# A two-layer float32 trunk: the order of its first loads, the place of a split before the down projection, and the engine of a layer norm's affine step

## The chip, the cores and the metric

One core of one Trainium2 chip runs the program. The metric is the device time of one execution in microseconds (us), as the median of several runs; smaller is better.

## The reference

The input is x with 256 positions of 2048 features, in float32. Two layers follow one another, each with a mixer and a feed-forward part, both with a residual add.

```
h = rms_norm(x, mix_norm[0]);  p = h @ ab_w_in                # 2048 x 6144
x = x + concat(band_attention(q, k, v, bias), b * conv(c * hv)) @ ab_w_out
x = x + (silu(g @ w_gate) * (g @ w_up)) @ w_down               # g = rms_norm(x, ffn_norm[0]), hidden width 5632
u, v = split(gelu(rms_norm(x, mix_norm[1]) @ c_w_in))          # 2048 x 4096
v = (v - mean) * rsqrt(var + eps) * ln_g + ln_b                # layer norm over the 2048 features
x = x + (u * (w_s @ v + b_s)) @ c_w_out
x = x + feed-forward as above, second weights
out = rms_norm(x, final_norm)
```

## The kernel before

**Matmuls in three terms.** Each float32 operand is split into a high part (a cast to FP32R on ScalarE) and a low part (the operand minus the high part, on VectorE). `three` (lines 478 to 481) issues three matmuls for each product: high by high (L479), high by low (L480), low by high (L481). The activations are the stationary operand (128 by 128), the weights the moving one (512 columns).

**Steps.** The whole program is a list of steps. A "std" step is one chunk of `RC` = 4 blocks of 128 contraction rows by 512 weight columns, 1 MB; it takes 4 blocks x 2 row halves x 3 terms = 24 matmuls. `load(t)` (L184) brings the weights of step t into one of three `raw` buffers on SyncE's (SP's) queue; `prep(t)` (L268) makes `whi` and `wlo` from them in two halves, `cast_half` (L258, ScalarE) and `low_part` (L264, VectorE), into two buffers each. `end_step(t)` (L521) calls `load(t + LOAD_AHEAD)` with `LOAD_AHEAD` = 4, and then `prep(t + PREP_AHEAD)` with `PREP_AHEAD` = 2, which loads step t + 2 itself if nothing has:

```
load(t + LOAD_AHEAD)
prep(t + PREP_AHEAD)
```

Phases follow each other in this list: ab_in (48 steps), ab_out, up0, down0, c_in, c_out, up1, down1.

**The start** (lines 614 to 666). Loads stand in the program in this order: half of x0, half of step 0's weights, the other half of x0, the other half of the weights, x1, step 1 (by `prep(1)`), x2, x3. Between them stand the split of step 0 in two halves of two blocks and the transposes of x (`x_transposes`, L395: eight TensorE transposes (L385) for one x block of 512 features, then `xh` on ScalarE and `xl` on VectorE). `later(dt, fn)` puts a piece of work into the program dt half steps later; `x_transposes` of x2 and x3 come at half steps 1 and 3. GpSimd (POOL) issues the loads of the norm vectors and of the attention bias (`load_bias`, L656).

**Order of instructions.** The tile framework orders each engine's instructions with its own model of time, except where `manual_schedule` holds ScalarE and VectorE to program order: here from the start to half step 9, and in `run_mixed` from its third step to its end.

**Up phases** (`run_mixed`, L537). Eight steps make one block of 512 hidden features, 11 blocks a phase; the steps' kinds are `MIX` = "NNSNSNSN". An S step uses sums of weight blocks, `tt` (`combine_first`, L228), and extra parts `ha`, `la`; these lie in the pool `mixw`, and the transposed activations in the pool `forms`. `WINDOWS` writes out which ScalarE and VectorE work goes into which step. At a block's end the PSUM banks are added up by VectorE in `first`, `end_a1`, `end_a2` and `end_b` (all through `add`, L864). After the last step of a phase the manual order is closed, `handover` (L905) closes both pools, opens `x_next` and `split`, and splits the first hidden tile with `hT.split(0)` (`jh` L208 on ScalarE, `jl` L209 on VectorE), and then `prep(hi_t + 1)` and the last block's `end_b`, `gate`, `product` follow. The down phase accumulates in two of the banks that `end_b` reads.

**Layer norm** (`layer_norm`, L954, in phase c_in). After mean and variance, each of eight blocks of `vt` (128 x 512) gets three VectorE instructions: (a + mu) * rs (L980, where `mu` is the negative mean), times `lng` (L984), plus `lnb` (L985). `spatial` (L990) multiplies the result on TensorE.

Of the kernel before, what the change touches and what calls it, by code (L numbers as in the profile page):

```python
# [16 lines left out]
P = 128  # L17
S = 256
# [57 lines left out]
def trunk_kernel(  # L76
# [35 lines left out]
    def close_pool(*names):  # L112
        for name in names:
            sides.pop(name).close()
# [69 lines left out]
    def load(t):  # L184
        if t >= len(steps) or t in raws:
            return
        s = steps[t]
        r = wpool.tile([P, RC, NB], F32, tag="raw", name="raw", bufs=RAW_BUFS)
        raws[t] = r

        def part(dst, w, c0, k, n):
            nc.sync.dma_start(
                dst, w[k * P : (k + n) * P, c0 : c0 + NB].rearrange("(k p) n -> p k n", p=P)
            )

        if s.kind != "std":
            for side, (w, c0) in enumerate(s.src):
                part(r[:, side::2, :], w, c0, s.k0, 2)
            return
        (w, c0), = s.src  # L200
        if t:
            part(r, w, c0, s.k0, RC)
        else:
            part(r[:, 0:2, :], w, c0, 0, 2)
            return lambda: part(r[:, 2:4, :], w, c0, 2, 2)

    def split(hi, lo, src):
        nc.scalar.copy(hi, src)  # L208
        nc.vector.tensor_tensor(out=lo, in0=src, in1=hi.bitcast(F32), op=ALU.subtract)  # L209
# [93 lines left out]
    def load_x(n, h=None):  # L303
        a, b = (0, NB) if h is None else (h * NB // 2, (h + 1) * NB // 2)
        nc.sync.dma_start(xs[n][:, :, a:b], xv[:, :, n * NB + a : n * NB + b])
# [57 lines left out]
    def rsqrt(dst, src):  # L363
        nc.gpsimd.tensor_tensor(out=dst, in0=src, in1=mhalf[:, : src.shape[1]], op=ALU.pow)
# [27 lines left out]
    def gain_col(st, c):  # L392
        return vcol(st.gain, c) if st.cols is None else st.cols[:, c : c + 1]

    def x_transposes(st, n):  # L395
        if st.mixed:
            for i in (2 * n, 2 * n + 1):
                x_forms(st, xs[n], i)
            return
        hi = st.pool[0].tile([P, 4, S], F32R, tag=f"xh{n}", name=f"xh{n}")  # L400
        lo = st.pool[0].tile([P, 4, S], F32R, tag=f"xl{n}", name=f"xl{n}")
        for half in range(2):
            pt = transpose_pair(xs[n], half * 2 * P)
            cols = [4 * n + half * 2 + j for j in range(2)]
            for j, c in enumerate(cols):
                nc.scalar.activation(
                    hi[:, c % 4, :], pt[:, j * S : (j + 1) * S], AF.Copy, scale=gain_col(st, c)
                )
            for j, c in enumerate(cols):
                nc.vector.scalar_tensor_tensor(  # L410
                    out=lo[:, c % 4, :], in0=pt[:, j * S : (j + 1) * S], scalar=gain_col(st, c),
                    in1=hi[:, c % 4, :].bitcast(F32), op0=ALU.mult, op1=ALU.subtract,
                )
        st.hi[n], st.lo[n] = hi, lo

    def x_forms(st, src, i):

# [116 lines left out]
        "N": ((2, NA11, "b", 1), (2, NA12, "b", 3), (5, NA21, "b", 0), (5, NA22, "b", 2),  # L534
              (3, NS3, "b", 0), (3, NS5, "b", 2), (4, NA21, "b", 1), (4, NA22, "b", 3)),
    }
    def run_mixed(pi, lhs, ends, handover):  # L537


        mixed[0] = True  # L540
        order = ExitStack()
        lo_t = cur[0]
        hi_t = lo_t
        while hi_t < len(steps) and steps[hi_t].pi == pi:
            hi_t += 1
        n = len(MIX)
        ps, seen, left = {}, set(), {}
        block_end = [None]

        def window(t, text):  # L550
            for word in text.split():
                op, _, dt = word.partition("+")
                tt = t + int(dt or 1)
                if op in ("c0", "c1", "s0", "s1", "s"):
                    if tt < hi_t and tt not in done:
                        (cast_half if op[0] == "c" else low_part)(tt, op[1:])
                elif dt:
                    if tt < hi_t:
                        assert steps[tt].kind == "S"
                        {"t1": combine_first, "t2": combine_rest, "ha": prep_a_hi,  # L560
                         "la": prep_a_lo}[op](tt)
                elif block_end[0] and op in block_end[0]:
                    block_end[0].pop(op)()

        done = set(parts)
        for t in range(lo_t, hi_t):
            if t == lo_t + 2:
                order.enter_context(
                    tc.manual_schedule(
                        engines={mybir.EngineType.Activation, mybir.EngineType.DVE}  # L570
                    )
                )
            s = steps[t]
            i = s.k0 // 2
            pre, _, post = WINDOWS[i].partition(":")
            window(t, pre)
            jobs_due(2 * t)
            if s.first:
                seen = set()
                left = {}  # L580
                for kind in MIX:
                    for q in PRODUCTS[kind]:
                        left[q[0]] = left.get(q[0], 0) + 1
            for j, (q, fa, group, slot) in enumerate(PRODUCTS[s.kind]):
                if j == 4:
                    jobs_due(2 * t + 1)
                if q not in seen:
                    ps[q] = bank(BANKS[q])
                hi, lo = (parts_a if group == "a" else parts)[t]
                left[q] -= 1  # L590
                three(ps[q], lhs.hi[i][:, fa, :], lhs.lo[i][:, fa, :], hi[:, slot, :],
                      lo[:, slot, :], q not in seen, left[q] == 0)
                seen.add(q)
            now[0] = 2 * t + 2
            if i == MIX.rindex("S"):
                block_end[0] = ends(s.key, ps)
            window(t, post)
            parts_a.pop(t, None)
            del parts[t]
            cur[0] += 1  # L600
            load(t + LOAD_AHEAD)
            if t + 2 == hi_t:
                prep(t + 2)
        order.close()
        handover()
        prep(hi_t + 1)
        for op in ("end_b", "gate", "product"):
            block_end[0].pop(op)()
        mixed[0] = False
# [16 lines left out]
    load_x(0, 1)  # L626
    load_second()
    load_x(1)
    hi0 = wpool.tile([P, RC, NB], F32R, tag="whi", name="whi", bufs=W_BUFS)
    lo0 = wpool.tile([P, RC, NB], F32R, tag="wlo", name="wlo", bufs=W_BUFS)  # L630
    for h in range(2):
        sl = slice(2 * h, 2 * h + 2)
        split(hi0[:, sl, :], lo0[:, sl, :], raws[0][:, sl, :])
        x_transposes(st, h)
    parts[0] = (hi0, lo0)
    prep(1)
    for n in (2, 3):
        load_x(n)
        later(2 * n - 3, lambda n=n: x_transposes(st, n))
    for n in range(4):  # L640
        later(3 + n, lambda n=n: squares(st, n))
# [21 lines left out]
        nc.gpsimd.memset(bt[0:CH, :, 0:CH], NEG)  # L663
        biases[g] = bt

    load_bias(0)

    def scaled(ps, dst):
        for m in range(M):
# [146 lines left out]
        else:  # L816
            grp["c", g] = dst

    def open_mixed():
        mixw[0] = open_pool("mixw", "left")  # L820
        xpool[0] = open_pool("forms", "left")

    def end_mix_a():
        close_pool("mix_a", "x_a")
        open_mixed()

    run(0, st, ab_in_evac)
    later(5, end_mix_a)
# [4 lines left out]
    class Hidden:  # L833
# [6 lines left out]
        def new(self, n):  # L840
            self.f[n] = self.pool.tile([P, 4, S], F32, tag=f"h{n}", name=f"h{n}")
            return self.f[n]

        def split(self, n):
            hi = self.split_pool.tile([P, 4, S], F32R, tag="jh", name="jh", bufs=2)
# [4 lines left out]
    def ffn(pi, st, nst):  # L850
# [52 lines left out]
                        product=product)  # L903

        def handover():  # L905
            close_pool("forms", "mixw")
            xpool[0] = open_pool("x_next", "left")
            hT.split_pool = open_pool("split", "left")
            operand[pi + 1] = hT
            hT.split(0)  # L910

        run_mixed(pi, st, ends, handover)
        if nst:
            run(pi + 1, hT, lambda n, ps: residual_evac(nst, n, ps))
        else:
# [16 lines left out]
    lnb = mpool.tile([P, D], F32, name="lnb")  # L932
    nc.gpsimd.dma_start(lng, c_ln_g[0:1, :].broadcast_to([P, D]))
    nc.gpsimd.dma_start(lnb, c_ln_b[0:1, :].broadcast_to([P, D]))
    ws = mpool.tile([P, G, P], F32, name="ws")
    nc.gpsimd.dma_start(ws, c_w_s[0].rearrange("g t s -> t g s"))
    wsT = mpool.tile([P, G, P], F32, name="wsT")
    vt = mpool.tile([P, M, D], F32, name="vt")
# [15 lines left out]
    def layer_norm():  # L954
# [17 lines left out]
        )  # L972
        rs = small.tile([P, M], F32, tag="rs", name="rs")
        rsqrt(rs, var)
        for n in range(4):
            sl = slice(n * NB, (n + 1) * NB)

            def block(m, sl=sl):
                a = vt[:, m, sl]
                nc.vector.tensor_scalar(  # L980
                    out=a, in0=a, scalar1=mu[:, m : m + 1], scalar2=rs[:, m : m + 1],
                    op0=ALU.add, op1=ALU.mult,
                )
                nc.vector.tensor_tensor(out=a, in0=a, in1=lng[:, sl], op=ALU.mult)  # L984
                nc.vector.tensor_tensor(out=a, in0=a, in1=lnb[:, sl], op=ALU.add)  # L985

            for m in range(M):
                later(1 + 2 * n + m, lambda m=m, block=block: block(m))
# [51 lines left out]

    def end_mix_c():
        close_pool("mix_c", "x_next")
        open_mixed()

    run(4, st_c, c_in_evac)
    later(5, end_mix_c)
# [62 lines left out]

    ffn(6, st_g, None)  # L1110
    drain()
    close_pool("x_next", "ffn")


# [28 lines left out]
```

## Time and profile before

| what | value |
|---|---|
| device time, median of 3 runs (lowest to highest) | 2102.51 us (2102.01 to 2103.68) |
| device time of the profiled execution | 2104.71 us |
| its span in the profile | 2102.7 us |
| TensorE matmul (PE) busy | 2080.8 us, 99% |
| VectorE (DVE) busy | 1503.7 us, 72% |
| ScalarE (ACT) busy | 1115.7 us, 53% |
| GpSimd (POOL) busy | 17.8 us, 1% |
| moved by DMA | 404.80 MB, 193 GB/s in the mean |

Durations in the profile belong to the one profiled execution; 2104.71 us is its own device time, and its span leaves out what lies around it. PE, DVE, ACT, POOL and SP stand for the five engines, PEld for TensorE's weight loads. "[1.85 <-ACT whi L258]" behind an instruction means that its engine stood idle for 1.85 us before it, until ScalarE had finished `whi` at line 258. Matmuls are pipelined: one's busy time runs into the next one's, so the pace is read from their starts.

### The profile page before, as it was taken

How to read it: one execution, taken by the hardware profiler on the slowest of the kernel's cores; microseconds unless marked ns; L12 is line 12 of the kernel's file. 1: busy time of each engine (PE TensorE's matmuls, PEld its weight loads, DVE VectorE, ACT ScalarE, POOL GpSimd, SP SyncE). 2: the span in 40 equal slices, each digit the busy share in tenths (PEclk: the TensorE clock that was granted, in tenths of full speed). 3: DMA queues.
4: the chain of work that ended last, by engine and by line, in shares of the span. 5: the costliest groups of instructions: out<-in, count | busy, mean ns of one | idle time of the engine just before them, and what ended most of it. 6: DMA issues, size and time to landing. Idle time of an engine off the chain costs nothing.

```text
span 2102.7 us, 24018 instructions
## 1 busy us (share of the span) xinstructions
PE 2080.8 (99%) x9356; PEld 1719.7 (82%) x9356; DVE 1503.7 (72%) x1597; ACT 1115.7 (53%) x1318; POOL 17.8 (1%) x37
## 2 busy tenths in 40 slices
PE   8999999999999999999999999999999999999998
PEld 6888888888888888788888878888888888878886
DVE  4445555788888888766664475588888888876675
ACT  5444445655555555556554534565555555555554
POOL 1000000000000000000000000000000000000000
PEclk9999999999999999999999999999999999999999
DMA  6554555565555555655555655556555655565554
GB/s 236 178 187 161 185 196 180 187 204 190 201 196 203 200 192 191 246 183 200 182 199 182 199 162 178 183 190 208 181 200 200 209 191 200 200 200 200 190 191 140
DMA packets 205345, 404.80 MB, mean 193 GB/s; under 512 B 9420, under 2 KB 10032, under 8 KB 204976
## 3 DMA queue, kind: packets, MB, share of 16 engines
q1 hardware_dynamic: 203296, 397.45, 55.8%
q0 software_dynamic: 1328, 4.77, 0.7%
q8 instruction: 73, 1.20, 0.2%
q10 hardware_dynamic: 608, 1.06, 0.1%
q14 instruction: 40, 0.33, 0.0%
HBM read 401.14 MB, written 2.10 MB: 192 GB/s over the span
## 4 chain that ended last, share of the span: by engine, by line
PE 96%; DMA 1%; DVE 1%; ACT 1%; issue 1%; SPq 0%; POOLq 0%; POOL 0%; ACTq 0%; DVEq 0%
PE b L481 31%; PE b L480 31%; PE b L479 31%; PE b L385 2%; DMA raw<-in_ab_w_in_dram 1%; PE b L421 0%; PE b L997 0%; DVE wlo L264 0%; ACT whi L258 0%; PE b L689 0%; ACT junk L965 0%; DVE vt L984 0%; DVE vt L980 0%; PE b L733 0%; PE b L721 0%
## 5 line engine op out<-in xcount | busy, mean ns | idle before, releaser
L264 DVE TENSOR_TENSOR wlo<-raw,whi 128x1024 fp32r<-128x1024 f32 x618 | 728.3, 1219 | 278.5 <-ACT whi L258 278.3
L258 ACT CAST whi<-raw 128x1024 fp32r<-128x1024 f32 x618 | 618.4, 1050 | 431.4 <-PE b L481 309.2
L480 PE MATMUL b<-wlo,fh 128*128 128x512 f32 x1144 | 449.2, 393 | 0.0
L481 PE MATMUL b<-whi,fl 128*128 128x512 f32 x1144 | 445.5, 389 | 0.0
L479 PE MATMUL b<-whi,fh 128*128 128x512 f32 x1144 | 380.6, 391 | 0.0
L481 PE MATMUL b<-whi,jl 128*128 128x512 f32 x704 | 274.3, 391 | 0.8 <-DVE jl L209 0.8
L480 PE MATMUL b<-wlo,jh 128*128 128x512 f32 x704 | 274.4, 390 | 0.4 <-DVE wlo L264 0.4
L480 PE MATMUL b<-wlo,xh 128*128 128x512 f32 x640 | 252.8, 395 | 2.9 <-DVE wlo L264 2.9
L479 PE MATMUL b<-whi,jh 128*128 128x512 f32 x704 | 249.8, 391 | 2.6 <-DVE sg L864 2.6
L481 PE MATMUL b<-whi,xl 128*128 128x512 f32 x640 | 251.5, 393 | 0.0
L481 PEld LDWEIGHTS b<-whi,fl 128*128 128x128 f32 x1144 | 214.9, 188 | 43.5
L480 PEld LDWEIGHTS b<-wlo,fh 128*128 128x128 f32 x1144 | 214.8, 188 | 43.4
L479 PEld LDWEIGHTS b<-whi,fh 128*128 128x128 f32 x1144 | 213.2, 188 | 45.1
L479 PE MATMUL b<-whi,xh 128*128 128x512 f32 x640 | 243.3, 399 | 1.9 <-ACT whi L258 1.9
L209 DVE TENSOR_TENSOR jl<-h,jh 128x1024 fp32r<-128x1024 f32 x88 | 107.8, 1225 | 148.5 <-ACT jh L208 148.5
L258 ACT CAST whi<-tt 128x1024 fp32r<-128x1024 f32 x132 | 134.7, 1052 | 124.9 <-PE b L481 96.2
L208 ACT CAST jh<-h 128x1024 fp32r<-128x1024 f32 x88 | 92.8, 1054 | 200.1 <-PE b L480 200.0
L264 DVE TENSOR_TENSOR wlo<-tt,whi 128x1024 fp32r<-128x1024 f32 x132 | 157.2, 1220 | 56.1 <-ACT whi L258 56.1
L479 PEld LDWEIGHTS b<-whi,jh 128*128 128x128 f32 x704 | 132.2, 188 | 31.1 <-ACT whi L258 3.4
L481 PEld LDWEIGHTS b<-whi,jl 128*128 128x128 f32 x704 | 132.6, 188 | 29.2 <-DVE jl L209 1.7
L480 PEld LDWEIGHTS b<-wlo,jh 128*128 128x128 f32 x704 | 132.6, 188 | 28.1 <-DVE wlo L264 0.8
L480 PEld LDWEIGHTS b<-wlo,xh 128*128 128x128 f32 x640 | 121.6, 190 | 28.9 <-DVE wlo L264 4.2
(148 smaller groups left out, 2054.8 us busy)
## 6 DMA issues: line engine op xcount, KB each, us to landing
raw<-in_ffn_w_gate_dram SPq DMA_DIRECT2D x176, 512.0 KB, 3.6
raw<-in_ffn_w_up_dram SPq DMA_DIRECT2D x176, 512.0 KB, 4.5
raw<-in_ffn_w_down_dram SPq DMA_DIRECT2D x88, 1024.0 KB, 4.9
raw<-in_ab_w_in_dram SPq DMA_DIRECT2D x47, 1024.0 KB, 5.0
raw<-in_c_w_in_dram SPq DMA_DIRECT2D x32, 1024.0 KB, 5.2
raw<-in_ab_w_out_dram SPq DMA_DIRECT2D x16, 1024.0 KB, 4.8
raw<-in_c_w_out_dram SPq DMA_DIRECT2D x16, 1024.0 KB, 4.9
x<-in_x_dram SPq DMA_DIRECT2D x3, 512.0 KB, 11.8
```

Source lines behind the costliest of these rows:

```text
L208: nc.scalar.copy(hi, src)
L209: nc.vector.tensor_tensor(out=lo, in0=src, in1=hi.bitcast(F32), op=ALU.subtract)
L258: nc.scalar.copy(parts[t][0][:, HALF[h], :], r[:, HALF[h], :])
L264: nc.vector.tensor_tensor(out=lo[:, sl, :], in0=r[:, sl, :], in1=hi[:, sl, :].bitcast(F32), op=ALU.subtract)
L385: nc.tensor.transpose(out=pt[:, j * S + m * P : j * S + (m + 1) * P], in_=src[:, m, c0 + j * P : c0 + (j + 1) * P], identity=ident,)
L479: nc.tensor.matmul(ps, lhsT=ah, rhs=bh, start=start, stop=False)
L480: nc.tensor.matmul(ps, lhsT=ah, rhs=bl, start=False, stop=False)
L481: nc.tensor.matmul(ps, lhsT=al, rhs=bh, start=False, stop=stop)
```

## The change

The first loads are put into the program as x0's first half, step 0's block 0, block 1, x0's second half, step 0's blocks 2 and 3, x1, step 1, x2, step 2, x3, and behind step 0's split step 3. The splits of step 0 become block 0, block 1, then blocks 2 and 3, with the transposes of x0 in two halves around them. `load_bias(0)` is called at half step 6. The first hidden tile's split stands in the program ahead of the last step of an up phase, still inside the manual order, and goes into a `tt` buffer of `mixw`, which therefore stays open from the first up phase to the program's end. `ws` shares `u`'s buffers. In the layer norm, (a + mu) * rs becomes a * rs + shift on ScalarE, with shift = mu * rs from one small VectorE instruction.

```diff
@@ load
-            part(r[:, 0:2, :], w, c0, 0, 2)
+            for k in range(2):
+                part(r[:, k : k + 1, :], w, c0, k, 1)
             return lambda: part(r[:, 2:4, :], w, c0, 2, 2)
@@ run_mixed
             pre, _, post = WINDOWS[i].partition(":")
+            if t + 1 == hi_t:
+                at_end()
             window(t, pre)
@@ start
     load_x(1)
+    for n in (1, 2):
+        load(n)
+        load_x(n + 1)
...
-    for h in range(2):
-        sl = slice(2 * h, 2 * h + 2)
-        split(hi0[:, sl, :], lo0[:, sl, :], raws[0][:, sl, :])
-        x_transposes(st, h)
+
+    def first_split(a, b):
+        split(hi0[:, a:b, :], lo0[:, a:b, :], raws[0][:, a:b, :])
+
+    x_transposes(st, 0, (0,))
+    first_split(0, 1)
+    first_split(1, 2)
+    x_transposes(st, 0, (1,))
+    first_split(2, 4)
+    x_transposes(st, 1)
     parts[0] = (hi0, lo0)
+    load(3)
     prep(1)
     for n in (2, 3):
-        load_x(n)
         later(2 * n - 3, lambda n=n: x_transposes(st, n))
...
-    load_bias(0)
+    later(6, lambda: load_bias(0))
@@ Hidden
+        def split_first(self):
+            both = mixw[0].tile([P, 2, 4, S], F32R, tag="tt", name="j0")
+            self.hi[0], self.lo[0] = both[:, 0], both[:, 1]
+            split(self.hi[0], self.lo[0], self.f[0])
@@ ffn
-            close_pool("forms", "mixw")
+            close_pool("forms")
             xpool[0] = open_pool("x_next", "left")
             hT.split_pool = open_pool("split", "left")
             operand[pi + 1] = hT
-            hT.split(0)
-
-        run_mixed(pi, st, ends, handover)
+
+        run_mixed(pi, st, ends, hT.split_first, handover)
@@ layer norm
-    ws = mpool.tile([P, G, P], F32, name="ws")
+    ws = mpool.tile([P, G, P], F32, tag="u", name="ws", bufs=2)
...
+        shift = small.tile([P, M], F32, tag="shift", name="shift")
+        nc.vector.tensor_tensor(out=shift, in0=mu, in1=rs, op=ALU.mult)
...
-                nc.vector.tensor_scalar(
-                    out=a, in0=a, scalar1=mu[:, m : m + 1], scalar2=rs[:, m : m + 1],
-                    op0=ALU.add, op1=ALU.mult,
+                nc.scalar.activation(
+                    a, a, AF.Identity, bias=shift[:, m : m + 1], scale=rs[:, m : m + 1]
                 )
```

The rest of the diff lets `x_transposes` take one half at a time, opens `mixw` once in `end_mix_a` and no more in `end_mix_c`, and closes it at the end.

## Rows read from the trace of the kernel before

**Rows 1.** The page, part 4: the chain that ended last, by engine

```profile
PE 96%; DMA 1%; DVE 1%; ACT 1%; issue 1%; SPq 0%; POOLq 0%; POOL 0%; ACTq 0%; DVEq 0%
```

**Rows 2.** Waits of PE: line, what it waited for, total us, times, longest us

```profile
PE b L480 <- DVE wlo L264: 3.3, 4, 1.9
PE b L479 <- DVE sg L864: 2.6, 2, 1.3
PE b L479 <- ACT whi L258: 1.9, 1, 1.9
PE b L481 <- DVE jl L209: 0.8, 2, 0.4
```

**Rows 3.** Windows: busy us (instructions) of PE, PEld, DVE, ACT, POOL; PEclk, DMA share, GB/s

```profile
30.00:32.00 2.00, 0.18 (x1) 0.19 (x2) 0.20 (x1) 1.28 (x2) 0.00 (x0) 1.00 0.03 11
855.00:865.00 10.00, 8.29 (x29) 5.97 (x28) 9.32 (x12) 4.89 (x6) 0.00 (x0) 0.85 0.99 364
1205.00:1225.00 20.00, 18.11 (x80) 14.74 (x79) 18.76 (x31) 8.85 (x12) 0.69 (x1) 1.00 0.49 157
1848.00:1862.00 14.00, 12.29 (x54) 9.40 (x53) 12.26 (x15) 7.45 (x9) 0.00 (x0) 1.00 0.68 229
```

**Rows 4.** The chain in order of time, 0 to 35 us: start us, us, what

```profile
10.99 11.18 DMA raw<-in_ab_w_in_dram
...
25.70 4.94 DMA raw<-in_ab_w_in_dram
```

**Rows 5.** Timeline of ACT, the first 12 us: start us, us, what, idle before

```profile
5.48 1.04 ACT L208 CAST whi<-raw 128x1024 fp32r<-128x1024 f32 x1 [2.97 <-DMA raw<-in_ab_w_in_dram]
```

**Rows 6.** Timeline of PE, the first 42 us

```profile
7.25 1.20 PE L479 MATMUL b<-whi,xh 128*128 128x512 f32 x2
...
23.34 0.73 PE L479 MATMUL b<-whi,xh 128*128 128x512 f32 x2
...
29.72 0.25 PE L336 MATMUL b<-ident,stage 96*128 96x96 f32 x1
31.82 0.73 PE L479 MATMUL b<-whi,xh 128*128 128x512 f32 x2 [1.85 <-ACT whi L258]
...
35.38 0.63 PE L480 MATMUL b<-wlo,xh 128*128 128x512 f32 x1
35.80 0.63 PE L481 MATMUL b<-whi,xl 128*128 128x512 f32 x1
...
41.11 0.62 PE L479 MATMUL b<-whi,xh 128*128 128x512 f32 x2
41.57 0.39 PE L480 MATMUL b<-wlo,xh 128*128 128x512 f32 x1
```

**Rows 7.** Timeline of all engines, 857 to 862 us, up0 to down0

```profile
857.26 0.69 DVE L864 TENSOR_TENSOR hh<-b,hh 128x512 f32<-128x512 f32 x1 [0.68 <-PE b L481]
...
859.66 0.68 DVE L864 TENSOR_TENSOR hh<-b,hh 128x512 f32<-128x512 f32 x1
...
859.89 0.47 PE L479 MATMUL b<-whi,jh 128*128 128x512 f32 x1 [1.31 <-DVE sg L864]
...
860.26 1.21 DVE L209 TENSOR_TENSOR jl<-h,jh 128x1024 fp32r<-128x1024 f32 x1
...
861.53 0.50 PE L481 MATMUL b<-whi,jl 128*128 128x512 f32 x1 [0.40 <-DVE jl L209]
```

**Rows 8.** Timeline of DVE, 1195 to 1240 us, the layer norm

```profile
1212.51 4.89 DVE L984 TENSOR_TENSOR vt<-vt,lng 128x512 f32<-128x512 f32 x8
```

**Rows 9.** Groups by line and shape: count | busy us, mean ns | idle before

```profile
L980 DVE TENSOR_SCALAR vt<-vt,mu,rs 128x512 f32<-128x512 f32 x8 | 3.7, 538 | 0.0
...
L890 ACT ACTIVATE sg<-sg,rstd 128x512 f32<-128x512 f32 x44 | 29.4, 716 | 0.0
...
L1017 ACT ACT_TABLE_LOAD x1 | 1.3, 1283 | 2.1 <-PE b L481 2.1
```

More of the change, by code (lines that the diff above doesn't have):

```diff
@@ L393, in gain_col, with x_transposes @@
         return vcol(st.gain, c) if st.cols is None else st.cols[:, c : c + 1]
-    def x_transposes(st, n):
+    def x_transposes(st, n, halves=(0, 1)):
         if st.mixed:
@@ L399, in x_transposes @@
             return
-        hi = st.pool[0].tile([P, 4, S], F32R, tag=f"xh{n}", name=f"xh{n}")
-        lo = st.pool[0].tile([P, 4, S], F32R, tag=f"xl{n}", name=f"xl{n}")
-        for half in range(2):
+        if n not in st.hi:
+            st.hi[n] = st.pool[0].tile([P, 4, S], F32R, tag=f"xh{n}", name=f"xh{n}")
+            st.lo[n] = st.pool[0].tile([P, 4, S], F32R, tag=f"xl{n}", name=f"xl{n}")
+        hi, lo = st.hi[n], st.lo[n]
+        for half in halves:
             pt = transpose_pair(xs[n], half * 2 * P)
@@ L413, in x_transposes @@
                 )
-        st.hi[n], st.lo[n] = hi, lo
     def x_forms(st, src, i):
@@ L536, in trunk_kernel, with run_mixed @@
     }
-    def run_mixed(pi, lhs, ends, handover):
+    def run_mixed(pi, lhs, ends, at_end, handover):
         mixed[0] = True
@@ L817, in ab_in_evac, with end_mix_a @@
             grp["c", g] = dst
-    def open_mixed():
+    def end_mix_a():
+        close_pool("mix_a", "x_a")
         mixw[0] = open_pool("mixw", "left")
         xpool[0] = open_pool("forms", "left")
-    def end_mix_a():
-        close_pool("mix_a", "x_a")
-        open_mixed()
     run(0, st, ab_in_evac)
@@ L1042, in end_mix_c @@
         close_pool("mix_c", "x_next")
-        open_mixed()
+        xpool[0] = open_pool("forms", "left")
     run(4, st_c, c_in_evac)
@@ L1111, in trunk_kernel @@
     drain()
-    close_pool("x_next", "ffn")
+    close_pool("x_next", "mixw", "ffn")
 _INS = ['x', 'mix_norm', 'ab_w_in', 'ab_rel_bias', 'ab_conv_w', 'ab_w_out', 'c_w_in', 'c_ln_g',
```

## The prediction

> **What bounds the kernel now.** First the chain that ended last: TensorE carries 96% of it [rows 1]. So the only question is where TensorE waits or runs slowly, and its own list of waits answers that [rows 2]: the largest are for `wlo`, `whi`, the bank adds of L864 and `jl`. By the stretches they lie at three places, and the change has a part for each.
>
> *The start.* From 30 to 32 us TensorE is busy for 0.18 us and the DMA engines for 3%, 11 GB/s [rows 3]: TensorE starves while the DMA idles. The chain shows why: one weight load takes from 10.99 us for 11.18 us, another from 25.70 for 4.94 [rows 4]. The code explains it. At the end of step 0 `load(4)` stands ahead of the `load(2)` inside `prep(2)`, so step 4 takes the third buffer, and steps 2 and 3 wait until step 0's and step 1's buffers are split. Queued behind step 1, x2, x3 and step 4, step 2 lands at 10.99 + 11.18 = 22.2 us. Step 3 takes a buffer only when step 2's own split is done at 25.7, and lands at 30.6. From 31.82 on matmuls start every 0.42 us (35.38, 35.80), and later every 0.23 us (two from 41.11, next at 41.57) [rows 6]: the lower clock level, after the wait.
>
> *The two hand-overs.* The first down matmul waits 1.31 us for VectorE's bank adds, the fifth 0.40 us more for `jl` [rows 7]; the waits of both hand-overs together are 2.6 and 0.8 us [rows 2].
>
> *The layer norm.* Between 1205 and 1225 us VectorE is busy for 18.76 of 20 us and ScalarE for 8.85 [rows 3]. VectorE takes eight L984 in a row from 1212.51 to 1217.4 [rows 8], and a low part that TensorE wants stands behind them: the 1.9 us that is the longest wait for `wlo` [rows 2].
>
> **The change part by part.** The sum is made against the profiled execution, 2104.71 us (span 2102.7 and about 2 us around it). The median of the runs, 2102.51, is 2.2 us lower, and I take the difference off that.
>
> *Order of the loads.* Steps 2 and 3 now get their buffers in turn. A step is 24 matmuls, at 0.23 us 5.5 us. Step 2 went from 23.34 to 29.72, 6.4 us: 0.9 us too long. Then came 1.85 us of waiting. Step 3 went from 31.82 to 41.11, 9.3 us: 3.8 us too long, at the lower clock [rows 6]. Together 6.5 us, if the loads come in time. By 22.2 us the queue had moved x (2.1 MB) and steps 0, 1, 4 and 2 (4.2 MB), 0.28 MB per us. Ahead of step 2 there are now x3 and step 4 less, 1.6 MB: it lands about 5.5 us earlier, near 16.7, x3 near 18.5, step 3 near 22. Step 2 is wanted at about 23, step 3 at 28 to 29: cover of 5 us or more each. ScalarE and VectorE keep program order here, and step 2's cast now stands with landed data ahead of x3's transposes. SP's queue holds step 3's load until step 0's split is done (about 11 us); behind it stands only step 4's, which has to wait for a later buffer anyway. Bounds: 0 to 6.9 us; I take 6.5, as each of the three pieces is a row.
>
> *First split in smaller pieces.* Today's first cast covers two blocks, starts at 5.48 and takes 1.04 [rows 5], and `xh` is behind it; the first matmul starts at 7.25 [rows 6]. Now `xh` comes first and the cast has half the columns, so half a cast, 0.5 us, comes off. But these matmuls run at the lower level, and if the clock rises at the same moment as before, only half of that is a gain: I take 0.3 (0 to 0.5). One more DMA issue on SP delays nothing, since the data queue is behind it. `load_bias(0)` is only moved in the program; on POOL nothing stands between, and nothing in the code holds it, so I expect its DMAs at the old time: 0.
>
> *Split of the first hidden tile.* `jh` was on ScalarE ahead of time before and stays so. `jl` (1.21 us) ran behind five bank adds; it now stands ahead of them on VectorE, which idles only 0.68 us there [rows 7]. So the adds come 1.21 - 0.68 = 0.53 us later and the first down matmul at 860.42 instead of 859.89. The second bank, whose add ended at 859.66 + 0.68, is free at about 861.0. In return nothing waits for `jl`: three matmuls on the first bank from 860.42, the fourth at about 861.1, the fifth at 861.3 instead of 861.53. That is 0.2 us for each hand-over, 0.4 in all. Bounds for each: a gain of 0.7, if the adds aren't pushed back (the fifth at 859.89 + 4 x 0.23 = 860.8), and a loss of 0.5, if nothing comes back; I take the 0.2 that the rows give. The wait for `jl` goes, and the adds are late next. `mixw` held open makes the pools behind it sit higher, so POOL's loads of `lng`, `lnb` and `ws` may go out at another time; at 855 to 865 us the DMA share is 0.99 and no row of PE's waits names a load [rows 2, 3], and the three are wanted hundreds of us later: 0.
>
> *Affine step on ScalarE.* VectorE loses eight L980 of 538 ns (3.7 us) and gains one tiny product; ScalarE gets eight activations of about 716 ns, 5.7 us (the nearest row: in place, 128 x 512, scale from a pointer) [rows 9]. ScalarE has 11 us free in those 20 [rows 3]. With 3.7 us less ahead of it, the low part is there about 1.8 us before TensorE wants it: 1.9 us gained. Bounds: all of it, or a loss of 1.4 (below).
>
> Sum: 6.5 + 0.3 + 0.4 + 1.9 = 9.1 us. 2104.7 becomes 2095.6 in a profile, and the median 2093.4.
>
> **Rivals.** *1, the layer norm's stall stays.* The framework orders ScalarE and VectorE here, and a run of eight activations could stand ahead of a cast, or the eight L984, now fed by ScalarE, still ahead of a low part. Per instruction ScalarE is slower, 716 against 538 ns [rows 9]: 8 x 0.18 = 1.4 us more on that path. With the stall as it was: 2095.3; with 1.4 more: 2096.7. Against it: VectorE was the full engine, ScalarE not half busy [rows 3]. The Trainium skill, ScalarE: Activation LUTs, section Rules for kernel authors, has multiplies and adds on VectorE and not on ScalarE; taken as the whole answer it gives the 2096.7, and the trace agrees with it for the single instruction only. Chance 0.20.
>
> *2, the clock.* The first hand-over ran at a mean granted clock of 0.85 over 10 us, the second at 1.00 over its stretch [rows 3], with alike waits: the first lost about 1.5 us by it. The gap ahead of the first down matmul grows to 1.8 us, as long as the 1.85 us after which step 3 lost 3.8 us [rows 6]. If both hand-overs lost 3.8: 2093.4 + 7.6 - 1.5 = 2099.5. For it: the equal gap; against it: as much work is done by the fifth matmul as before. The Trainium skill, TensorE: Matmul & The Clock Gate, section What's actually happening, says that the gate's count runs on freely and doesn't start with the kernel, so that the same gap may or may not be hit; the two hand-overs agree. If the first keeps its clock: 2091.9. Chance of the bad case 0.06.
>
> *3, the start is only half cured.* x3's transposes stand on TensorE's queue, and x3 now lands behind step 2; if TensorE reaches them first, it waits there and the clock falls after all. Then the 3.8 us and the 0.3 stay lost: 2097.5. For it: TensorE's order comes from a model of time. Against: x3 near 18.5 us. Chance 0.07.
>
> *4, slower.* `Identity` is a function that this kernel hasn't used. If it needed a table other than the casts, each of the eight blocks would pay a reload there and back, 16 x 1.283 = 20.5 us, and 5.7 us of activations [rows 9], against 11.15 us free on ScalarE [rows 3]: 15 us of TensorE's time in place of 1.9, which makes 2108.5. It decides from about eleven reloads on, where the 9.1 us are used up. Against it: Gelu, copies and casts follow each other in this phase with one load at L1017 [rows 9]. Chance 0.04.
>
> **How the numbers follow.** Forecast 0.63, rivals 0.20, 0.06, 0.07 and 0.04. The range takes in the forecast with the first hand-over at full clock and a better split (2091.0) and rival 1 with its worst price and a little more (2097.2); outside lie rivals 2 and 4 and about half of 3. A measurement of this kernel can tell about 0.2% from no change, 4.2 us: faster is below 2098.3. Forecast and rivals 1 and 3 are faster, 0.90; rival 2 is the same, 0.06; rival 4 slower, 0.04.
>
> **What would show it.** Right: no row of TensorE waiting for `whi` in the first 45 us, step 4's first matmul near 34 instead of 41.11, the DMA near its full rate until 20 us or so; the first down matmul 0.5 us later after the last up matmul than before, and no wait for `jl`; no wait for `wlo` near 1210; table loads as many as before. Wrong: a granted clock below 1 after 13 us at the start, a wait for x's transposes, a wait for `whi` near 1210, or clock lows at both hand-overs. A slower time would disprove the reading that TensorE's waits are the whole of it.

## The result: 1.8% slower, with fewer waits than before

The changed kernel takes 2142.18 us (median of 6, 2141.75 to 2142.77); the kernel before, on the same chip, 2103.1 us (6 runs). The ratio is 1.0184, with an interval from 1.0171 to 1.0197. The forecast was 2093.4 us, in a range from 2091.0 to 2097.2.

The profile after, 2140.0 us long, is read in the order of the prediction. First TensorE's list of waits (line waited for, total in us, times, longest), which answers to [rows 2]:

```profile
PE b L626 <- DMA first<-in_mix_norm_dram: 3.5, 1, 3.5
PE b L386 <- DMA x<-in_x_dram: 3.5, 1, 3.5
PE b L481 <- DVE sg L879: 3.0, 2, 1.5
PE b L482 <- DVE wlo L265: 0.3, 1, 0.3
```

Two waits at the very start stood in the list of before as well:

```profile
PE b L622 <- DMA first<-in_mix_norm_dram: 3.7, 1, 3.7
PE b L385 <- DMA x<-in_x_dram: 1.3, 1, 1.3
```

Nothing waits for `whi` or `jl` any more, and the waits for `wlo` are down to 0.3 us; the wait for x grew by 2.2 us and those for the bank adds by 0.4. The whole list goes from 13.6 to 10.3 us. Two stretches to be read against [rows 3] (us, busy time of PE, PEld, DVE, ACT and POOL with instructions; then granted clock, DMA share, GB/s), the same one at the start, and the first hand-over, which now lies between 868 and 878 us:

```profile
30.00:32.00 2.00, 2.00 (x11) 1.59 (x10) 0.91 (x2) 1.94 (x5) 0.00 (x0) 1.00 0.13 17
868.00:878.00 10.00, 8.49 (x37) 6.55 (x36) 10.00 (x12) 5.13 (x6) 0.00 (x0) 1.00 0.54 168
```

From 30 to 32 us TensorE was busy for 0.18 us before and is busy throughout now; at the hand-over it has its full clock. The chain that ended last, by engine, against [rows 1]:

```profile
PE 98%; DVE 1%; issue 0%; DMA 0%; ACT 0%; SPq 0%; POOLq 0%; POOL 0%; DVEq 0%
```

TensorE has 98% of the chain, where it had 96%. So TensorE waits 3.3 us less, and the time is 39 us longer: the matmuls themselves must be slower. TensorE's costliest groups of instructions (line, engine, operation, output and inputs, shapes, count, then busy us and mean ns of one) say so. The kernel before:

```profile
L480 PE MATMUL b<-wlo,fh 128*128 128x512 f32 x1144 | 449.2, 393 | 0.0
L480 PE MATMUL b<-wlo,jh 128*128 128x512 f32 x704 | 274.4, 390 | 0.4 <-DVE wlo L264 0.4
L480 PE MATMUL b<-wlo,cath 128*128 128x512 f32 x128 | 49.8, 389 | 0.0
```

and after:

```profile
L482 PE MATMUL b<-wlo,fh 128*128 128x512 f32 x1144 | 454.8, 398 | 0.0
L482 PE MATMUL b<-wlo,jh 128*128 128x512 f32 x688 | 272.3, 396 | 0.3 <-DVE wlo L265 0.3
L482 PE MATMUL b<-wlo,cath 128*128 128x512 f32 x128 | 49.8, 389 | 0.0
```

The same matmul with the same shapes takes 5 or 6 ns more where its stationary tile is `fh` (up phases) or `jh` (down phases), and exactly as long as before where it is `cath` (ab_out). The pace, from the starts in TensorE's timeline (start, us busy), before:

```profile
900.24 0.39 PE L480 MATMUL b<-wlo,jh 128*128 128x512 f32 x1
900.47 0.39 PE L481 MATMUL b<-whi,jl 128*128 128x512 f32 x1
900.70 0.39 PE L479 MATMUL b<-whi,jh 128*128 128x512 f32 x1
900.92 0.39 PE L480 MATMUL b<-wlo,jh 128*128 128x512 f32 x1
```

and after:

```profile
900.28 0.40 PE L482 MATMUL b<-wlo,jh 128*128 128x512 f32 x1
900.52 0.39 PE L483 MATMUL b<-whi,jl 128*128 128x512 f32 x1
900.75 0.40 PE L481 MATMUL b<-whi,jh 128*128 128x512 f32 x1
900.98 0.39 PE L482 MATMUL b<-wlo,jh 128*128 128x512 f32 x1
```

From the first start to the fourth it is 0.68 us before, 0.227 for each matmul, and 0.70 us after, 0.233. It is not the clock and not the DMA. The stretch from 440 to 820 us, all inside up0, before:

```profile
440.00:820.00 380.00, 380.00 (x1711) 314.04 (x1710) 327.64 (x331) 206.54 (x216) 0.00 (x0) 1.00 0.59 199
```

and after:

```profile
440.00:820.00 380.00, 380.00 (x1671) 305.91 (x1670) 319.89 (x322) 201.01 (x210) 0.00 (x0) 1.00 0.57 193
```

In both TensorE is busy all the time at a granted clock of 1.00, and the DMA engines have room; after, it gets 40 matmuls fewer done. The loss is spread over the whole program, and by phase (from the first matmul of a phase to the first of the next, in down1 to the start of the last matmul; out of TensorE's timeline, us) it stands beside e1, the changed kernel with its stationary tiles put back in their place, which is explained below:

| phase | before | after | e1 | after - e1 |
|---|---|---|---|---|
| up to the first matmul | 7.25 | 9.32 | 7.66 | 1.66 |
| ab_in | 293.44 | 292.24 | 287.28 | 4.96 |
| ab_out | 90.68 | 90.73 | 90.68 | 0.05 |
| up0 | 468.52 | 480.21 | 468.88 | 11.33 |
| down0 | 245.48 | 249.97 | 243.08 | 6.89 |
| c_in | 187.92 | 190.50 | 186.17 | 4.33 |
| c_out | 90.68 | 90.71 | 90.68 | 0.03 |
| up1 | 468.52 | 480.21 | 468.88 | 11.33 |
| down1 | 241.62 | 247.64 | 240.83 | 6.81 |

A whole phase of 1056 matmuls (down: 44 steps of 24) loses 6.8 us, 6.4 ns each; ab_out and c_out lose next to nothing.

### The profile page after: what moved, and what is told of

Its sections match the earlier page's. It is cut to its first block, busy times and chain, and to the rows that moved or that the text cites. A ratio compares the mean times of both kernels' runs of the same rounds, so it can differ in the third digit from the quotient of the medians.

```text
span 2140.0 us, 24018 instructions
## 1 busy us (share of the span) xinstructions
PE 2121.4 (99%) x9356; PEld 1715.4 (80%) x9356; DVE 1500.9 (70%) x1591; ACT 1119.6 (52%) x1327; POOL 17.8 (1%) x37
## 4 chain that ended last, share of the span: by engine, by line
PE 98%; DVE 1%; issue 0%; DMA 0%; ACT 0%; SPq 0%; POOLq 0%; POOL 0%; DVEq 0%
PE b L481 32%; PE b L482 32%; PE b L483 32%; PE b L386 2%; PE b L423 0%; PE b L1012 0%; DMA x<-in_x_dram 0%; DVE wlo L265 0%; PE b L702 0%; DVE sg L879 0%; PE b L746 0%; PE b L734 0%; PE b L749 0%; DVE j L210 0%; DVE hh L879 0%
## 5 line engine op out<-in xcount | busy, mean ns | idle before, releaser
L482 PE MATMUL b<-wlo,fh 128*128 128x512 f32 x1144 | 454.8, 398 | 0.0
L483 PE MATMUL b<-whi,fl 128*128 128x512 f32 x1144 | 451.3, 394 | 0.0
L481 PE MATMUL b<-whi,fh 128*128 128x512 f32 x1144 | 386.5, 396 | 0.0
L210 DVE TENSOR_TENSOR jl<-h,jh 128x1024 fp32r<-128x1024 f32 x86 | 105.2, 1225 | 157.3 <-ACT jh L209 154.8
L483 PEld LDWEIGHTS b<-whi,xl 128*128 128x128 f32 x640 | 120.4, 188 | 28.6
```

Source lines behind the costliest of these rows:

```text
L481: nc.tensor.matmul(ps, lhsT=ah, rhs=bh, start=start, stop=False)
L482: nc.tensor.matmul(ps, lhsT=ah, rhs=bl, start=False, stop=False)
L483: nc.tensor.matmul(ps, lhsT=al, rhs=bh, start=False, stop=stop)
```

## The experiments

**What the slow phases share.** Their stationary tiles (`xh`, `fh`, `jh` and the low parts) lie in pools of the left side of SBUF that stand behind the pool `small`. The change puts one new tile into `small`: `shift`, which takes 64 bytes of each partition and moves all of those pools up by 64. `cath` and `ush`, the stationary tiles of ab_out and c_out, lie on the right side, and the weights in `wpool`, ahead of `small`; these stay. Three fillers of the kernel set the places:

```
small.tile([P, SMALL_PAD // 4], F32, name="small_pad", bufs=1)    # SMALL_PAD = 256
right.tile([P, RIGHT_PAD // 4], F32, name="right_pad")            # RIGHT_PAD = 992
const.tile([P, CONST_PAD // 4], F32, name="const_pad")            # CONST_PAD = 928
```

By the sizes of the tiles in the source (a count, with small tiles rounded up to 32 bytes; no view shows addresses), the first `xh` begins 52224 bytes behind the first `whi` in the kernel before, 204 x 256. SMALL_PAD moves the stationary tiles alone, CONST_PAD the weights and the stationary tiles, RIGHT_PAD those of the right side. The theory is that the place sets the pace; the rival is that the change's own work or order does.

**e1, the changed kernel with the 64 bytes taken back.**

```
-SMALL_PAD = 256
+SMALL_PAD = 192
```

> The changed kernel with SMALL_PAD 192 instead of 256: the new tile shift takes 64 bytes in the pool small, and the smaller pad moves every pool behind it (forms, mixw, x_a, x_next, split) back by 64 bytes, to the addresses of before, a multiple of 1024. Theory A (the slower matmul pace of the changed kernel comes from this shift of the stationary tiles): about 8058 of 8826 wide matmuls go back from 0.233 to 0.227 us, 49 us less: 2093 us, and the start spacing is 0.227 in every phase. Theory B (the pace comes from the change's own work or from its new order): stays at 2142 us with 0.233.

Measured: 2094.25 us (5 runs, 2094.05 to 2094.61) against 2102.61, ratio 0.9958 [0.9946, 0.9971]. The groups are back where they were:

```profile
L482 PE MATMUL b<-wlo,fh 128*128 128x512 f32 x1144 | 449.3, 393 | 0.0
L482 PE MATMUL b<-wlo,jh 128*128 128x512 f32 x688 | 267.9, 389 | 0.4 <-DVE wlo L265 0.4
```

One number of filler is worth 2142.18 - 2094.25 = 47.9 us, all of the slowdown and more. So no instruction, wait or order of the change is needed to explain the loss.

**e2, the kernel before with 64 bytes more.**

```
-SMALL_PAD = 256
+SMALL_PAD = 320
```

> The kernel before with SMALL_PAD 320 instead of 256, nothing else: the same pools move up by 64 bytes, as in the changed kernel. Theory A: 8058 wide matmuls at 0.233 instead of 0.227 us, 2103 + 49 = 2152 us; ab_out and c_out, whose stationary tiles lie in pools that do not move, keep 0.227. Theory B: 2103 us, 0.227 everywhere.

Measured: 2148.49 us, ratio 1.0218 [1.0202, 1.0234]. The loss appears without any of the change.

**e3, the kernel before with 512 bytes more.**

```
-SMALL_PAD = 256
+SMALL_PAD = 768
```

> The kernel before with SMALL_PAD 768: the same pools move up by 512 bytes. If a stationary slice (512 bytes in each partition) must only start at a multiple of 512: 2103 us and 0.227. If it is the multiple of 1024 that counts: 2152 us and 0.233. Theory B: 2103 us.

Measured: 2102.35 us, ratio 0.9996 [0.9986, 1.0006]. It is not that the tiles moved, nor a pool that got tight, but by how many bytes they moved.

**e4, weights moved and stationary tiles not.**

```
-CONST_PAD = 928
-SMALL_PAD = 256
+CONST_PAD = 992
+SMALL_PAD = 192
```

> The kernel before with CONST_PAD 992 and SMALL_PAD 192: raw, whi, wlo and x move up by 64 bytes, the pools with the stationary tiles stay. If only the stationary operand's address counts: 2103 us, 0.227. If the moving operand's counts as well: slower in all phases, ab_out and c_out too, by about 50 us. Theory B: 2103 us.

Measured: 2123.54 us (2 runs), ratio 1.0097 [1.0079, 1.0116]; up0 473.73 us. Slower too, though no stationary tile has moved, but by 21 us, less than half of e2's loss: neither of the two times that were expected. And ab_out, whose stationary tiles hadn't moved either, rose from 90.68 to 91.46.

**The parts of the change, each alone in the kernel before.** p_start has the order of the loads and the smaller first splits:

```
-            part(r[:, 0:2, :], w, c0, 0, 2)
+            for k in range(2):
+                part(r[:, k : k + 1, :], w, c0, k, 1)
...
+    for n in (1, 2):
+        load(n)
+        load_x(n + 1)
```

> Only the start of the change (order of the first loads, first split in three pieces, load_bias moved), no new tile, so every address as before. Theory A (the parts pay as their stretches in the realigned kernel show, and only the address shift cost time): the stretch up to ab_out is 5.8 us shorter, 2102.6 becomes 2096.8 us; step 4 begins near 35 instead of 41. Theory C (the start's gain comes only together with the other parts, or is given back later): within 1 us of 2102.6.

Measured: 2099.65 us (11 runs, 2096.95 to 2101.89) against 2102.79, ratio 0.9984 [0.9975, 0.9993]. That is 3.1 us of the 5.8 that were expected. The execution in the profile took 2097.45 us, and up to ab_out it is as short as e1; what the longer ones lost was not recorded.

p_norm has the affine step on ScalarE, with the filler cut so that nothing moves:

```
-SMALL_PAD = 256
+SMALL_PAD = 192
...
+        shift = small.tile([P, M], F32, tag="shift", name="shift")
+        nc.vector.tensor_tensor(out=shift, in0=mu, in1=rs, op=ALU.mult)
```

> Only the layer norm's affine step on ScalarE, with SMALL_PAD 192 so that the tile shift moves nothing. Theory A: the 1.9 us wait for wlo near 1216 us shrinks to 0.2 or so, 2102.6 becomes 2100.9 us. Theory C: 2102.6, with a wait for whi or wlo in the same place.

Measured: 2100.59 us, ratio 0.9991 [0.9982, 0.9999].

p_split has the first hidden tile's split in the last step, with `mixw` held open:

```
+            if t + 1 == hi_t:
+                at_end()
             window(t, pre)
...
-            close_pool("forms", "mixw")
+            close_pool("forms")
```

> Only the split of the first hidden tile ahead of the last up step, with mixw held open and ws in u's buffers; every stationary tile starts at a multiple of 1024 as before. Theory A: the first down matmul comes 0.36 us later at each hand-over and the wait for jl is gone; 0.4 us gained for each, 2101.8 us, and 1.6 us more if the first hand-over keeps its clock (2100.2). Theory C (the reordered hand-over loses): 2103 to 2104.

Measured: 2100.74 us, ratio 0.9990 [0.9981, 0.9999]. Each part gains, the last two by intervals that only just leave out no change; the medians add up to 3.1 + 2.2 + 2.05 = 7.4 us, and e1 with all three gained 8.4. `mixw` held open moves the pools behind it, `x_next` and `split`, by its 20480 bytes (80 x 256, counted from the source) without harm: down0 is 243.11 us in p_split and 243.86 in e3. (c_in is 189.49 us, 1.6 longer than before; the granted clock is 0.83 there from 1215 to 1225 us, as in both64 below.)

**Own address or distance.** If the weights or the stationary tiles had to begin at certain bytes, moving both by 64 would be slow twice; if their distance counts, it would be free.

```
-CONST_PAD = 928
+CONST_PAD = 992
```

> The kernel before with CONST_PAD 992: weights and stationary tiles on the left both move by 64 bytes. If each operand's own address counts: the two losses add, 46 + 21 = 67 us, 2169 us. If it is their distance from each other that counts: 2102.6 us. If the slower of the two readings hides the other: 2148 us.

Measured: 2107.47 us, ratio 1.0019 [1.0009, 1.003], with up0 at 468.85 us. The distance counts. The profiled execution of both64 is still 6.4 us longer than that of e3 (spans 2107.0 and 2100.6 us). Of these 1.6 are in ab_out and c_out (91.47 each): the right side did not move with the weights. Another 0.7 are in the two up phases. And 3.2 are the clock, in c_in (189.62 us against 187.9) and down1 (243.12 against 241.59); the last 0.9 lie at the start and behind the last matmul. Here is the stretch around the layer norm's 1.9 us wait for `wlo`, in both64 and then in e3 (columns as above):

```profile
1215.00:1225.00 10.00, 8.10 (x29) 6.20 (x28) 10.00 (x15) 3.34 (x5) 0.00 (x0) 0.83 0.48 159
1215.00:1225.00 10.00, 8.51 (x38) 7.09 (x39) 10.00 (x15) 4.20 (x5) 0.00 (x0) 1.00 0.34 111
```

At the second hand-over, from 1853 to 1863 us, both64 has a granted clock of 0.83 again. So one and the same wait may or may not be followed by a stretch at the lower of the two clock levels, and when it is, 1.5 to 1.7 us more are lost.

The other way round, right64 moves the right side alone, by 64 bytes:

```
-RIGHT_PAD = 992
+RIGHT_PAD = 1056
```

> The kernel before with RIGHT_PAD 1056: only the tiles of the right side move, by 64 bytes; of the stationary ones these are cat and us, used in ab_out and c_out alone. Theory A (the stationary slice's own address sets the pace): ab_out and c_out take 90.68 + 384 x 0.006 = 93.0 us each, all other phases as before: 2102.6 + 4.6 = 2107.2 us. If instead any shift of the memory's contents, or of the pools on the left as a whole, did it: 2102.6, or much more than 4.6 us.

Measured: 2105.77 us, ratio 1.0012 [1.0003, 1.0022]; ab_out 91.41 and c_out 91.43 us, up0 468.60. The effect is confined to the moved side, as expected, and smaller than expected: 0.7 us a phase in place of 2.3. If the right side is filled from its far end, a larger filler moves its tiles down, and the distance is 192 modulo 256, as in e4, where ab_out lost 0.8. No run shows the direction; the price fits 192 and not 64. (c_in is 189.62 us here too, with a granted clock of 0.83 from 1215 to 1225 us.)

**The scale.** Three more distances, by SMALL_PAD = 384 (q128), 448 (q192) and 512 (q256b) in the kernel before:

```
-SMALL_PAD = 256
+SMALL_PAD = 384
```

> The kernel before with SMALL_PAD 384: the left pools move by 128 bytes. If a stationary slice must start at a multiple of 64 x an odd number to be slow (128 is enough): 2102.6 and 0.227. If it must start at a multiple of 256 or 512: 2148 us and 0.233.

> The kernel before with SMALL_PAD 448: stationary tiles on the left up by 192 bytes. If the distance counts modulo 256, this is the case of the weights moved by 64: up phases 473.7 us, 2122 us. If not: near 2146 us, as for 64 and 128.

> The kernel before with SMALL_PAD 512, stationary tiles on the left up by 256 bytes. If the distance counts modulo 256: up phases 468.5 us, 2102.6 us. If only multiples of 512 are free: 480 us and 2148 us.

An earlier run of the same edit as q256b, q256, had one execution of 2102.15 us, in line with it, and one of 10960.51 us with a granted clock of 0.18, which says nothing about the distance. The last of these runs is cross, which has the distance 64 at other addresses:

```
-CONST_PAD = 928
-SMALL_PAD = 256
+CONST_PAD = 992
+SMALL_PAD = 320
```

> The kernel before with CONST_PAD 992 and SMALL_PAD 320: weights up by 64 bytes, stationary tiles on the left up by 128, so 64 apart as in the changed kernel. If the distance counts: up phases 480 us, ab_out and c_out 91.4, together 2149 us. If each operand's own address counts: 128 for the stationary (2146) and 64 for the weights (21 more): 2167 us.

All together, with the moves in bytes and the distance from the start of `whi` to the start of the stationary tiles modulo 256:

| run | weights | stationary | distance | up0, us | device time, us | ratio |
|---|---|---|---|---|---|---|
| before | 0 | 0 | 0 | 468.52 | 2102.5 | 1 |
| q256b | 0 | 256 | 0 | 468.53 | 2102.89 | 0.9999 [0.9988, 1.001] |
| e3 | 0 | 512 | 0 | 468.52 | 2102.35 | 0.9996 [0.9986, 1.0006] |
| both64 | 64 | 64 | 0 | 468.85 | 2107.47 | 1.0019 [1.0009, 1.003] |
| e2 | 0 | 64 | 64 | 479.97 | 2148.49 | 1.0218 [1.0202, 1.0234] |
| cross | 64 | 128 | 64 | 479.82 | 2151.93 | 1.0235 [1.0205, 1.0265] |
| q128 | 0 | 128 | 128 | 478.88 | 2145.8 | 1.0202 [1.0182, 1.0223] |
| q192 | 0 | 192 | 192 | 473.88 | 2120.68 | 1.0086 [1.0057, 1.0115] |
| e4 | 64 | 0 | 192 | 473.73 | 2123.54 | 1.0097 [1.0079, 1.0116] |

The up phase falls into the same class whenever the distance does, whatever the addresses: 468.5 to 468.9, 479.8 to 480.0, 478.9, 473.7 to 473.9. The changed kernel, at distance 64, has 480.21, of which about 0.4 is its later hand-over.

Could ScalarE and VectorE, which read and write the same weights, be what TensorE collides with? From the start times of up0 (400 to 850 us), matmuls on `whi` and `wlo` start every 233.3 ns in e2 also where both engines stand idle (64 intervals), against 226.7 ns before (32). So they are not needed for the loss. But the distance to `whi` is not the whole of it either: a group of matmuls in the up phases streams `ha` and `la` out of `mixw`, which keep their distance to `fh` in e2 and in e4, and yet the 198 of `ha` with `fl` went from 389 to 393 ns in both. Why is open.

**b1, the change without its loss.** It writes the product into `mu` instead of a new tile, loads x0's second half ahead of the second block of weights, and splits the first hidden tile one step earlier (the main lines):

```
-        shift = small.tile([P, M], F32, tag="shift", name="shift")
-        nc.vector.tensor_tensor(out=shift, in0=mu, in1=rs, op=ALU.mult)
+        nc.vector.tensor_tensor(out=mu, in0=mu, in1=rs, op=ALU.mult)
...
-            part(r[:, 0:2, :], w, c0, 0, 2)
-            return lambda: part(r[:, 2:4, :], w, c0, 2, 2)
+            part(r[:, 0:1, :], w, c0, 0, 1)
+            return lambda k, n: part(r[:, k : k + n, :], w, c0, k, n)
...
-            if t + 1 == hi_t:
-                at_end()
             window(t, pre)
+            if t + 2 == hi_t:
+                at_end()
```

> The changed kernel, but shift is written into mu's tile, so that the pool small keeps its size and all addresses are those of before; x0's second half is loaded ahead of block 1 of step 0; and the first hidden tile is split one step earlier, behind that step's own casts and low parts. Theory A: as the realigned kernel, 2094.25, less about 0.4 at the start and 0.4 at each hand-over: 2093 us, all matmuls at 0.227. If the earlier split delays the low parts of the last up step: a wait for wlo there and 2094 to 2096. Theory B (the pace comes from the change's work): 2142.

Measured: 2093.31 us (5 runs, 2092.78 to 2093.39) against 2102.79, ratio 0.9953 [0.9941, 0.9966]. The first product starts at 7.08 us, and the first down matmul waits no longer than before (1.31 us, [rows 7]), with no wait for `jl`:

```profile
852.08 0.39 PE L482 MATMUL b<-whi,fl 128*128 128x512 f32 x1
853.78 0.47 PE L480 MATMUL b<-whi,j 128*128 128x512 f32 x1 [1.31 <-DVE sg L879]
854.09 0.40 PE L481 MATMUL b<-wlo,j 128*128 128x512 f32 x1
```

It is faster than both kernels.

## Why the prediction was wrong

**The failed step** is in "Affine step on ScalarE": VectorE "gains one tiny product". It was priced as an instruction, at nothing. The product's result needs a tile, the tile moves every stationary tile behind it by 64 bytes against the weights, and that cost 47.9 us (after against e1), or 46.1 in the kernel before (e2 against e3). The same gap is in "Split of the first hidden tile", where the move of the pools behind `mixw` was noticed and weighed by its DMA times alone; there the move happens to be harmless (p_split). None of the four rivals was a pace of the matmuls. Rival 4 looked for a slower time on ScalarE, and that did not come: four table loads before and four after. (Its 2108.5 also leaves the layer norm's 1.9 us in as a gain; without them it is 2110.4.) "A slower time would disprove the reading that TensorE's waits are the whole of it" was the line that held: TensorE was busy for 99% of the time before, and a busy TensorE was taken for one at a fixed pace, 0.23 us for each matmul.

The other terms can be read from e1, where the pace is the old one.

**Order of the loads, right, and its first end wrong.** Up to ab_out e1 gains 293.44 + 7.25 - 287.28 - 7.66 = 5.75 us; predicted were 6.5 + 0.3. How much it is depends on the clock of the execution that it is measured against: before, the granted clock from 30 to 40 us was 0.66; in right64, with the old order and a like wait for `whi` (1.8 us), it was 1.00, and against that run e1 gains only 3.8 us. Steps 2 and 3 run without a wait, step 4 begins at about 35.4 us instead of 41.11 (predicted: near 34). But the first product comes later, not earlier. TensorE's timeline of e1, to be read against [rows 6]:

```profile
6.93 1.08 PE L386 MATMUL b<-ident,x 128*128 128x128 f32 x4 [1.38 <-DMA x<-in_x_dram]
7.66 1.20 PE L481 MATMUL b<-whi,xh 128*128 128x512 f32 x2
...
17.00 0.63 PE L386 MATMUL b<-ident,x 128*128 128x128 f32 x4 [0.92 <-DMA x<-in_x_dram]
```

and of the changed kernel:

```profile
8.58 1.09 PE L386 MATMUL b<-ident,x 128*128 128x128 f32 x4 [3.52 <-DMA x<-in_x_dram]
9.32 1.20 PE L481 MATMUL b<-whi,xh 128*128 128x512 f32 x2
...
12.33 0.39 PE L481 MATMUL b<-whi,xh 128*128 128x512 f32 x1
12.56 0.39 PE L482 MATMUL b<-wlo,xh 128*128 128x512 f32 x1
```

TensorE's order has the transposes of x0's second half ahead of the first product, and that half now comes behind two loads of weights. "First split in smaller pieces" priced the cast (a gain of 0.3) and not the load that TensorE waits for. The first product starts 2.1 us later than before in the changed kernel and 1.7 in p_start (8.98 us). e1's 0.4 is within the spread, as runs of the old order start between 7.13 and 8.08 us. Little of the loss stays, since these matmuls start 0.43 us apart until about 12 us in either kernel, and 0.23 after. Rival 3 is there in small: the 0.92 us wait is for an x block, and the clock does not fall behind it.

**Hand-overs, right.** `jl` is waited for no longer. The first down matmul of e1 waits 1.67 us in place of 1.31:

```profile
852.44 0.39 PE L483 MATMUL b<-whi,fl 128*128 128x512 f32 x1
854.50 0.47 PE L481 MATMUL b<-whi,j 128*128 128x512 f32 x1 [1.67 <-DVE sg L879]
```

That is 0.36 us later (predicted 0.53). At the second hand-over up1 is 0.36 us longer and down1 0.79 shorter: 0.43 gained (predicted 0.2). The first gives the same against runs of the old order that kept their clock there: 243.86 (e3) to 243.08 us for down0, less 0.36. The kernel before had 245.48 in its profile; those 1.6 us are the clock of [rows 3], which neither e3 nor q256b shows. Rival 2 did not come: the changed kernel has a granted clock of 1.00 at both hand-overs (868 to 878 and 1880 to 1894 us).

**Layer norm, right.** c_in is 187.92 - 186.17 = 1.75 us shorter in e1 and in p_norm (predicted 1.9). ScalarE in e1 (timeline), and TensorE's wait behind it:

```profile
1200.12 5.76 ACT L996 ACTIVATE vt<-vt,shift,rs 128x512 f32<-128x512 f32 x8 [0.41 <-DVE shift L990]
...
1205.79 1.99 ACT L259 CAST whi<-raw 128x1024 fp32r<-128x1024 f32 x2
```
```profile
1210.84 0.49 PE L482 MATMUL b<-wlo,xh 128*128 128x512 f32 x1 [0.17 <-DVE wlo L265]
```

Rival 1's order came true: the eight activations stand in a row ahead of a cast. But of the stall 0.17 us is left. An activation took about 800 ns, not the estimated 716, against 538 on VectorE [rows 9]:

```profile
L996 ACT ACTIVATE vt<-vt,shift,rs 128x512 f32<-128x512 f32 x8 | 5.8, 803 | 0.4 <-DVE shift L990 0.4
```

The Trainium skill, ScalarE: Activation LUTs, section Rules for kernel authors, which would keep multiplies and adds off ScalarE, holds here for the instruction and not for the kernel: VectorE was the full engine (18.76 of 20 us busy, [rows 3]), and the move gained 1.75 us.

Together, in spans, e1 gains 2102.7 - 2092.6 = 10.1 us: 5.75 at the start, 1.75 in the layer norm, 0.4 at each hand-over and the 1.6 of the clock, 9.9; in medians 8.4, against 9.1 predicted. That these lie so close is in part luck: the start gave a good microsecond less than forecast, and the 1.6 us of the clock, which the forecast did not count, made up for it. What is left open is why x0's second half came 2 us later in the changed kernel than in e1.

## What to carry to other kernels

A new tile is a part of a change: before pricing its instruction, ask which pools stand behind it and whether the stationary and the moving operands of the matmuls keep their distance. When a change removes waits and the time rises, compare the mean of like matmul groups and the starts within one phase before looking for a new wait. When a gain rests on the clock falling behind a wait, look at several executions, since it falls in some and not in others. And test the parts of a change at the old placement, or a loss that belongs to none of them will be put down to one.

## What the hardware showed that was not expected

The pace of this kernel's 128 x 128 by 512 matmuls changes with the place of the stationary tiles in SBUF relative to the weights `whi` and `wlo`. At distances of 0, 256 and 512 bytes from the old one an up phase takes 468.5 us, at 64 480.0, at 128 478.9, at 192 473.9, all at a granted clock of 1.00. In a down phase of 1056 matmuls these are 6.4 ns each for 64 (248.39 us in e2 against 241.59 in e3) and 2.1 for 192 (243.83 in q192). Moving both leaves the pace (468.9 us). The Trainium skill, SBUF — State Buffer, section Operand start alignment, asks for starts at a multiple of the element size, which every run here keeps, and calls that legality, not speed; here the place costs over 2% (e2 and cross). A conflict between the reads of the next stationary tile and of the moving operand would fit most of this, though not the matmuls on `ha` and `la`; no run here shows where it arises, and distances that aren't a multiple of 64 were not tried.
